# A two-layer diffusion backbone with mixture of experts: order and depth of the expert weight loads

## Chip, cores and metric

The kernel runs on one core of one Trainium2 chip. The metric is the device time of one execution in microseconds (us), the median of several runs.

## What is computed

A latent sequence `x` and a context sequence, 256 tokens of width 1024 each, go through two layers. Each layer mixes tokens with gated recurrences (`token_mix`) and then mixes channels: in layer 0 with a dense SwiGLU, in layer 1 with the two best of eight experts. All of it is float32. The last part, layer 1's channel mix on the 256 latent tokens, is where the change lies:

```python
def swiglu(h, w1, w3, w2):
    return (jax.nn.silu(h @ w1) * (h @ w3)) @ w2

def moe_swiglu(h, router, w1, w3, w2):
    t = h.reshape(b * l, d)
    logits = (t @ router).astype(jnp.float32)
    top_v, top_i = lax.top_k(logits, TOP_K)          # 2 of 8
    top_w = jax.nn.softmax(top_v, axis=-1)
    gates = jnp.sum(jax.nn.one_hot(top_i, N_EXPERTS) * top_w[..., None], axis=1)
    y = jnp.zeros_like(t)
    for e in range(N_EXPERTS):                       # D_EXPERT = 3584
        y = y + gates[:, e:e + 1] * swiglu(t, w1[e], w3[e], w2[e])
```

## The kernel before

Up to about 993 us the kernel does layer 0, layer 1's token mix and its output projection (`w_out`). Then come the experts, to which everything below belongs.

**Experts and steps.** The kernel ranks the experts on the chip by how many tokens chose them; only the expert of rank 0 is fixed beforehand (expert 0). Ranks 1 to 4 are "big" (up to 128 tokens), ranks 0, 5, 6 and 7 "small" (up to 64). An expert's 3584 hidden columns are cut into 7 pieces, so there are 56 steps (r, c), 28 big and 28 small. The list `steps` begins with three small ones (rank 0, pieces 0 to 2), then alternates big and small, and ends with four big ones in a row. The loop at L1233 runs one step n after the other: up projection of step n (`up_big` or `up_small`), `silu` on ACT and the product on DVE (tile `a`), then the down projection of step n-1 (`lower`), then the transposes of `a` on PE. Below, up(n) and lower(n) are these two projections of step n.

**Weights.** A step needs 6 tiles of 1 MB (`w`): four for the up projection, two for the down projection, 336 tiles in all. They are numbered here from 0 in the order in which the plan has them: up(0) has tiles 0 to 3, up(1) 4 to 7, lower(0) 8 and 9, up(2) 10 to 13, lower(1) 14 and 15, up(3), the first big one, 16 to 19. All loads are issued from SP's queue in this order. Each goes into the next buffer of a ring (`raw_ring`, L880) of 12: two of the pool `raws`, which the pieces of `w_out` used before, nine of `pre`, whose memory belonged to layer 1's token mix, and one of `late`. A load waits until what its buffer held has been used, and every load behind it in the queue waits with it. A tile is two pieces. For a small step PE reads the pieces as they are. For a big step each piece is split into a rounded half and a remainder: `wh` on ACT, then `wl` on DVE, into a ring of four pairs of buffers (`spl_ring`).

**Lookahead.** Each engine runs its instructions strictly in the order in which the program issues them. `taken_pieces` decides where in that order loads and splits stand: when PE's work on piece i is issued, the pieces after it are issued too, up to `LOOK` of them or until three split ones stand ahead:

```python
while (len(emitted) <= i or len(emitted) <= i + LOOK and sum(len(x) == 2 for x in emitted[i + 1:]) < 3) \
        and next(feeder, 0) is None:
    pass
```

`EARLY` (L854) is how many pieces of the experts' tiles are issued while `w_out` still runs.

**Gathers.** Tokens are gathered for an expert by matmuls with a one-hot matrix `P`, which DVE builds (`onehot`). For rank 0 this happens ahead of the steps, in the loop at L1027: for each quarter q of the width, `token_lo(q)` makes the remainder half `htkl` of the tokens on DVE, PE gathers, ACT and DVE take the result (`xgs`). Behind the loop `order_experts` computes on DVE which expert has which rank (`whoi`). SP then reads `whoi` into registers with seven TENSOR_LOADs (`read_order`, L998), since the loads of all other ranks take their addresses from there. For the groups of ranks 1 to 4 `open_group(g)` builds `P` at step 0, 11, 25 and 30, and four gathers stand in the down projections that are issued in that step and the three behind it (for group 1, in steps 1 and 2, two each).

Of the kernel before, what the change touches and what calls it, by code (L numbers as in the profile page):

```python
# [27 lines left out]
BIG, SMALL = (1, 2, 3, 4), (0, 5, 6, 7)  # L28
NPRE = 9
AHEAD = 2  # L30
LOOK = 16
EARLY = 1


def body(ctx, tc, I, out, dbg=None):
# [25 lines left out]
    raws = pool("raws", 2)  # L61
# [28 lines left out]
    raw_ring = {"n": 0, "pools": [(raws, 2)]}  # L90
# [720 lines left out]
    pre = pool("pre", NPRE, side="right")  # L811
# [41 lines left out]

    limit[0] = taken[0] + 8 + EARLY - 1  # L854
    w_out(1, 0, to_tokens)
# [21 lines left out]

    mp = pool("mp", 1, side="left")
    late = pool("late", 1, side="left")
    raw_ring.update(n=0, pools=[(raws, 2), (pre, NPRE), (late, 1)])  # L880
    spl_ring.update(n=0, pools=[(spl, 3), (spx, 1)])
    gt = mp.tile([128, 2, NE, NE], F32, name="gt")
    eq = mp.tile([128, 2, NE, NE], F32, name="eq")
# [21 lines left out]
    def token_lo(q):  # L905
        c = slice(256 * q, 256 * q + 256)
        for tt in range(2):
            DVE.scalar_tensor_tensor(htk[1][:, tt, c], x2t[:, tt, c], r2[:, tt:tt + 1], htk[0][:, tt, c].bitcast(F32),
                                     op0=ALU.mult, op1=ALU.subtract)
# [77 lines left out]
    def order_experts():  # L987
        DVE.tensor_copy(cnt, counts)
        DVE.scalar_tensor_tensor(key, cnt, 8.0, seq, op0=ALU.mult, op1=ALU.subtract)
        DVE.memset(key[:, 0:1], 8192.0)  # L990
        DVE.tensor_tensor(cmp_, key[:, None, :].to_broadcast(sq8), key[:, :, None].to_broadcast(sq8), op=ALU.is_gt)
        DVE.tensor_reduce(rk, cmp_, axis=AX.X, op=ALU.add)
        DVE.tensor_tensor(place, rk[:, None, :].to_broadcast(sq8), seq[:, :, None].to_broadcast(sq8), op=ALU.is_equal)
        DVE.tensor_mul(cmp_, place, seq[:, None, :].to_broadcast(sq8))
        DVE.tensor_reduce(who, cmp_, axis=AX.X, op=ALU.add)
        DVE.tensor_copy(whoi, who)
# [27 lines left out]

    xgs[0] = small_tile()
    limit[0] = None
    for q in range(4):  # L1027
        token_lo(q)
        b = bank(("po", "pp")[q % 2])
        for a in range(2):  # L1030
            k = 2 * q + a
            o = b[:, 64 * a:64 * a + 64]
            for i in range(2):
                for tt in range(2):
                    mm(o, htk[i][:, tt, 128 * k:128 * k + 128], hot[0][:, tt, 0:64], i + tt == 0, i + tt == 2)
            if a:
                DVE.tensor_scalar(xgs[0][:, k], o, amp[:, k:k + 1], shift[:, k:k + 1], op0=ALU.mult, op1=ALU.add)
            else:
                ACT.activation(xgs[0][:, k], o, AF.Identity, scale=amp[:, k:k + 1], bias=shift[:, k:k + 1])
    order_experts()  # L1040

    def up_big(ws, xg):
# [93 lines left out]
    def open_group(g):  # L1136
        if len(members(g)) == 2:
            hot[g] = onehot([posr[:, :, g:g + 1], posr[:, :, g + 4:g + 5]], [128, 64])
            xgs[g], xgs[g + 4] = big_tiles(), small_tile()
        else:  # L1140
            hot[g] = onehot([posr[:, :, g:g + 1]], [128])
            xgs[g] = big_tiles()
# [27 lines left out]
    def taken_pieces(n):  # L1170
# [3 lines left out]
        def at(k):  # L1174
            i = first + k
            while (len(emitted) <= i or len(emitted) <= i + LOOK and sum(len(x) == 2 for x in emitted[i + 1:]) < 3) \
                    and next(feeder, 0) is None:
# [1 line left out]
            return tuple(x[:, 0] for x in emitted[i])  # L1179
        return at  # L1180

    before, mids, after = {}, {}, {}

    def at_step(table, n, f):
        table.setdefault(n, []).append(f)
# [7 lines left out]
    n = -5  # L1193
    for g in BIG:
        free = {2: (0,), 3: (1, 5), 4: (2,)}.get(g, ())
        n = max([n + 5] + [1 + steps.index((r, 6)) for r in free])
        assert all(n + (3 if g == 1 else 4) <= steps.index((r, 0)) for r in members(g)), (g, n)
        at_step(before, n, lambda g=g: open_group(g))
        for k in range(0, KT, 2):
            at_step(mids, n + 1 + k // 4 if g == 1 else n + k // 2, lambda g=g, k=k: gather_group(g, k))  # L1200
        at_step(mids, n + 4, lambda g=g: back_group(g))
# [12 lines left out]
    def scatter():  # L1214
        if not jobs:
            return []
        r, t, cuts = jobs.pop(0)
        y = halves(t)
        return [lambda rows=rows, i=i, tt=tt: spill(y, rows, back[r], gate_of(r), i, tt)
                for rows, i in cuts for tt in range(2)]  # L1220
# [12 lines left out]
    for n, (r, c) in enumerate(steps):  # L1233
        if n == len(steps) - 6:
            gf = sb(mp, [128, KT, 128], F32R, "xgh", 2).rearrange("p a b -> p (a b)").bitcast(F32)
            SP.dma_start(gf, I["fg"].partition_broadcast(128))
        rest = scatter()
        a = up_big(taken_pieces(KT), xgs[r]) if r in BIG else up_small(taken_pieces(KT), xgs[r])
        for f in before.pop(n, []):
            f()  # L1240
        rest += mids.pop(n, [])
        if prev is not None:
            lower(*prev, rest)
        prev = (r, c, (turn_big if r in BIG else turn_small)(a))
        for f in after.pop(n, []):
            f()
# [154 lines left out]
```

## Time and profile before

| | |
|---|---|
| Median of 3 runs | 1923.0 us (1922.17 to 1924.91) |
| The profiled execution, its own time | 1919.4 us |
| Its span (first to last instruction) | 1917.6 us |
| PE busy, share of the span | 95 % |
| DVE, ACT busy | 63 %, 50 % |
| DMA, mean over the span | 258 GB/s |

Rows give times from the span's start. PE is TensorE (matmuls), PEld its weight loads, DVE VectorE, ACT ScalarE, POOL GpSimd, SP SyncE, SPq its queue of DMA issues. "[x <-Y]" in a timeline says that the engine stood idle for x us before the instruction and that Y ended it. Matmuls are pipelined, so a busy PE need not be PE at its peak. Most instructions are recorded by one helper, so they all have line L47; the names of the tiles tell them apart.

### The profile page before, as it was taken

The page shows a single profiled execution, that of the slowest core. Times are in us where ns is not written, and L with a number is a line of the kernel's source. Part 1 is how long each engine was busy: PE and PEld are TensorE (multiplying, and loading weights), DVE is VectorE, ACT ScalarE, POOL GpSimd, SP SyncE. Part 2 cuts the span into 40 slices and gives each one's busy share as a digit, 9 for nine tenths or more (in the row PEclk, how much of TensorE's full clock was granted, in tenths as well). Part 3 has the DMA queues.
Part 4 walks back from the last instruction along what each step waited for, and adds up shares of the span by engine and source line. Part 5 has one row for each costly group of instructions (what it writes and reads, how often), then busy time and mean ns, then how long its engine had stood idle before and what let it go on. Part 6 is the DMA issues. An engine that isn't in the chain of part 4 may idle for free.

```text
span 1917.6 us, 30283 instructions
## 1 busy us (share of the span) xinstructions
PE 1830.0 (95%) x11901; PEld 1330.4 (69%) x11901; DVE 1206.3 (63%) x1923; ACT 951.3 (50%) x1506; POOL 49.4 (3%) x94
## 2 busy tenths in 40 slices
PE   6999999999999999999995999999999999999995
PEld 4887778988888888987882466565646565565574
DVE  5799985789774346657751465556646565665485
ACT  4757664532122236666650555444546464454464
POOL 0111100000000001000100000000000000000000
PEclk9999999999999999999998999999999999999998
DMA  9344213366773323311238999999999999999990
GB/s 353 120 148 149 72 47 110 144 229 209 254 269 124 110 95 118 109 45 68 93 107 336 421 422 421 373 405 421 421 408 383 404 396 421 420 421 421 421 412 27
DMA packets 76731, 495.10 MB, mean 258 GB/s; under 512 B 8448, under 2 KB 10752, under 8 KB 23072
## 3 DMA queue, kind: packets, MB, share of 16 engines
q1 hardware_dynamic: 76576, 493.03, 65.4%
q8 instruction: 97, 1.59, 0.3%
q14 instruction: 58, 0.48, 0.1%
HBM read 491.95 MB, written 1.05 MB: 257 GB/s over the span
## 4 chain that ended last, share of the span: by engine, by line
PE 80%; DMA 7%; DVE 6%; ACT 5%; issue 2%; SPq 0%; ACTq 0%; DVEq 0%
PE pj L47 63%; PE po L47 11%; PE pp L47 6%; DMA w<-in_mw 4%; ACT wh L47 1%; ACT kpad L47 1%; DVE junk L47 1%; DMA raw<-in_win 1%; DVE wl L47 1%; ACT ptd L47 1%; DMA wg<-in_wgroup 1%; DMA wm<-in_wmod 1%; DVE Q L47 0%; DVE nt L47 0%; ACT F L47 0%
## 5 line engine op out<-in xcount | busy, mean ns | idle before, releaser
L47 DVE TENSOR_TENSOR wl<-w,wh 128x1024 fp32r<-128x1024 f32 (+1 forms) x501 | 602.1, 1215 | 243.7 <-ACT wh L47 229.2
L47 ACT ACTIVATE wh<-w 128x1024 fp32r<-128x1024 f32 (+1 forms) x501 | 522.3, 1050 | 380.0 <-PE pj L47 279.0
L47 PE MATMUL pj<-hh,wh 128*128 128x512 f32 (+1 forms) x992 | 349.4, 353 | 1.7 <-ACT hh L47 1.0
L47 PE MATMUL pj<-hh,wl 128*128 128x512 f32 (+1 forms) x992 | 347.8, 351 | 1.6 <-DVE wl L47 1.6
L47 PE MATMUL pj<-hl,wh 128*128 128x512 f32 (+1 forms) x992 | 348.7, 352 | 0.5 <-DVE hl L47 0.5
L47 PE MATMUL pj<-w,xgs 128*64 128x512 f32 x896 | 202.5, 603 | 5.8 <-DMA w<-in_mw 5.8
L47 PEld LDWEIGHTS pj<-hh,wh 128*128 128x128 f32 x992 | 186.5, 188 | 30.2 <-issue 3.4
L47 PEld LDWEIGHTS pj<-hl,wh 128*128 128x128 f32 x992 | 186.8, 188 | 27.5 <-issue 2.5
L47 PEld LDWEIGHTS pj<-hh,wl 128*128 128x128 f32 x992 | 186.7, 188 | 26.7 <-DVE wl L47 2.5
L47 DVE SCALAR_TENSOR_TENSOR junk<-wm,cbc 128x1024 bf16<-128x1024 f32 x128 | 156.4, 1222 | 41.1 <-DMA wm<-in_wmod 40.1
L47 PE MATMUL pj<-wh,xgh 128*128 128x512 f32 x448 | 179.8, 401 | 0.0
L47 PE MATMUL pj<-wl,xgh 128*128 128x512 f32 x448 | 177.7, 397 | 0.0
L47 PE MATMUL pj<-wh,xgl 128*128 128x512 f32 x448 | 177.6, 396 | 0.0
L47 DVE TENSOR_TENSOR a<-a,pj 128x256 f32<-128x256 f32 (+1 forms) x78 | 45.8, 589 | 171.6 <-ACT a L47 165.5
L47 PEld LDWEIGHTS pj<-w,xgs 128*64 128x64 f32 x896 | 62.2, 139 | 126.1 <-issue 111.3
L47 ACT ACTIVATE a<-pj 128x256 f32<-128x256 f32 (+1 forms) x78 | 40.0, 513 | 189.8 <-PE pj L47 189.6
L47 PE MATMUL pj<-w,aT 128*64 128x512 f32 x448 | 109.5, 618 | 0.6 <-DMA w<-in_mw 0.6
L47 PEld LDWEIGHTS pj<-wh,xgl 128*128 128x128 f32 x448 | 84.4, 188 | 20.3
L47 PEld LDWEIGHTS pj<-wl,xgh 128*128 128x128 f32 x448 | 84.5, 189 | 19.8 <-DVE wl L47 0.7
L47 PEld LDWEIGHTS pj<-wh,xgh 128*128 128x128 f32 x448 | 84.4, 188 | 19.2
L47 PE MATMUL po<-wh,aTh 128*128 128x512 f32 x224 | 93.3, 417 | 0.7 <-ACT aTh L47 0.7
L47 PE MATMUL po<-wh,aTl 128*128 128x512 f32 x224 | 88.8, 396 | 0.0
(273 smaller groups left out, 2446.7 us busy)
## 6 DMA issues: line engine op xcount, KB each, us to landing
w<-in_mw SPq DMA_DIRECT2D x336, 1024.0 KB, 11.7
wm<-in_wmod SPq DMA_DIRECT2D x80, 512.0 KB, 4.2
w<-in_win SPq DMA_DIRECT2D x31, 1024.0 KB, 4.8
w<-in_fw SPq DMA_DIRECT2D x30, 1024.0 KB, 4.9
w<-in_wout SPq DMA_DIRECT2D x12, 1024.0 KB, 4.8
wg<-in_wgroup SPq DMA_DIRECT2D x8, 1024.0 KB, 14.5
w<-in_fw SPq DMA_DIRECT2D x8, 768.0 KB, 4.3
xT<-in_ctxT SPq DMA_DIRECT2D x1, 1024.0 KB, 8.1
```

The costliest lines, as they stand in the source:

```text
L47: ins = fn(*args, **kw)
```

## The change

Four edits. The ring of 12 buffers begins with the nine of `pre` and not with the two of `raws`. The lookahead is 6 pieces and not 16, and no expert tile is issued while `w_out` runs. `token_lo` runs two quarters ahead of the gathers that need it. And `open_group` of the groups 2 to 4 is issued at the beginning of its step, ahead of the up projection, not behind it.

```diff
--- before.py
+++ after.py
@@ -28,8 +28,8 @@
 BIG, SMALL = (1, 2, 3, 4), (0, 5, 6, 7)
 NPRE = 9
 AHEAD = 2
-LOOK = 16
-EARLY = 1
+LOOK = 6
+EARLY = 0
 
 
 def body(ctx, tc, I, out, dbg=None):
@@ -877,7 +877,7 @@
 
     mp = pool("mp", 1, side="left")
     late = pool("late", 1, side="left")
-    raw_ring.update(n=0, pools=[(raws, 2), (pre, NPRE), (late, 1)])
+    raw_ring.update(n=0, pools=[(pre, NPRE), (late, 1), (raws, 2)])
     spl_ring.update(n=0, pools=[(spl, 3), (spx, 1)])
     gt = mp.tile([128, 2, NE, NE], F32, name="gt")
     eq = mp.tile([128, 2, NE, NE], F32, name="eq")
@@ -1024,8 +1024,9 @@
 
     xgs[0] = small_tile()
     limit[0] = None
+    token_lo(0)
+    token_lo(1)
     for q in range(4):
-        token_lo(q)
         b = bank(("po", "pp")[q % 2])
         for a in range(2):
             k = 2 * q + a
@@ -1037,6 +1038,8 @@
                 DVE.tensor_scalar(xgs[0][:, k], o, amp[:, k:k + 1], shift[:, k:k + 1], op0=ALU.mult, op1=ALU.add)
             else:
                 ACT.activation(xgs[0][:, k], o, AF.Identity, scale=amp[:, k:k + 1], bias=shift[:, k:k + 1])
+        if q < 2:
+            token_lo(q + 2)
     order_experts()
 
     def up_big(ws, xg):
@@ -1179,7 +1182,7 @@
             return tuple(x[:, 0] for x in emitted[i])
         return at
 
-    before, mids, after = {}, {}, {}
+    early, before, mids, after = {}, {}, {}, {}
 
     def at_step(table, n, f):
         table.setdefault(n, []).append(f)
@@ -1195,7 +1198,7 @@
         free = {2: (0,), 3: (1, 5), 4: (2,)}.get(g, ())
         n = max([n + 5] + [1 + steps.index((r, 6)) for r in free])
         assert all(n + (3 if g == 1 else 4) <= steps.index((r, 0)) for r in members(g)), (g, n)
-        at_step(before, n, lambda g=g: open_group(g))
+        at_step(early if n else before, n, lambda g=g: open_group(g))
         for k in range(0, KT, 2):
             at_step(mids, n + 1 + k // 4 if g == 1 else n + k // 2, lambda g=g, k=k: gather_group(g, k))
         at_step(mids, n + 4, lambda g=g: back_group(g))
@@ -1234,6 +1237,8 @@
         if n == len(steps) - 6:
             gf = sb(mp, [128, KT, 128], F32R, "xgh", 2).rearrange("p a b -> p (a b)").bitcast(F32)
             SP.dma_start(gf, I["fg"].partition_broadcast(128))
+        for f in early.pop(n, []):
+            f()
         rest = scatter()
         a = up_big(taken_pieces(KT), xgs[r]) if r in BIG else up_small(taken_pieces(KT), xgs[r])
         for f in before.pop(n, []):
```

What this does to the order on the engines, at three places. First SP's queue, from the last load of `w_out` (`in_wout`) on, before the change; in brackets stands which engine's or DMA queue's count an issue waits for:

```order
L47 DMA w_10063<-in_wout 128x2048 [waits DMAHW1_49,DVE_49]
L47 DMA w_10135<-in_mw 128x2048 [waits DMAHW2_49,DVE_49]
L47 DMA w_10354<-in_mw 128x2048 [waits DMAHW4_49,DVE_49]
L47 DMA w_10356<-in_mw 128x2048 [waits DMAHW5_49,PE_49]
L47 DMA w_10358<-in_mw 128x2048 [waits Pool_49]
L47 DMA w_10360<-in_mw 128x2048 [waits Pool_49]
L47 DMA w_10362<-in_mw 128x2048
L47 DMA w_10364<-in_mw 128x2048 [waits DMAHW3_49]
L47 DMA w_10366<-in_mw 128x2048
```

Four more loads follow until the first TENSOR_LOAD of `whoi`: twelve tiles stand ahead of it. The same queue from the same load on, changed:

```order
L47 DMA w_10063<-in_wout 128x2048 [waits DMAHW1_49,DVE_49]
L47 DMA w_10352<-in_mw 128x2048 [waits Pool_49]
L47 DMA w_10354<-in_mw 128x2048 [waits Pool_49]
L47 DMA w_10356<-in_mw 128x2048
L47 DMA w_10358<-in_mw 128x2048
L47 DMA w_10364<-in_mw 128x2048
L47 DMA w_10370<-in_mw 128x2048 [waits DMAHW2_49]
L47 DMA w_10376<-in_mw 128x2048 [waits DMAHW3_49]
L1000 TENSOR_LOAD whoi [waits DVE_49]
```

The wait for PE, which the third load had, is gone: these tiles all go to `pre`. The first TENSOR_LOAD, which waits for DVE, now stands behind seven tiles.

Second DVE around tile 16, the first that is split; ACT has the halves `wh` of the same pieces at the same places. Before the change (`wl_10527` and `wl_10549` are tile 16, `wl_10573` is tile 17; `xgl` belongs to the gathers of group 1; `a_10520` and `a_10602` are the steps 1 and 2):

```order
L47 TENSOR_TENSOR a_10520<-a_10520,pj_10495 128x256
L47 TENSOR_TENSOR wl_10527<-w_10524,wh_10526 128x1024
L47 TENSOR_TENSOR xgl_10481<-g_10541,xgh_10480 128x256
L47 TENSOR_TENSOR wl_10549<-w_10524,wh_10548 128x1024
L47 TENSOR_TENSOR xgl_10481<-g_10563,xgh_10480 128x256
L47 TENSOR_TENSOR wl_10573<-w_10570,wh_10572 128x1024
L47 TENSOR_TENSOR a_10602<-a_10602,pj_10585 128x256
L47 TENSOR_TENSOR xgl_10481<-g_10616,xgh_10480 128x256
```

The same place, changed (`wl_10585` and `wl_10591` are tile 16, `wl_10602` is tile 17; `a_10510` and `a_10596` are the steps 1 and 2):

```order
L47 TENSOR_TENSOR a_10510<-a_10510,pj_10485 128x256
L47 TENSOR_TENSOR xgl_10471<-g_10527,xgh_10470 128x256
L47 TENSOR_TENSOR xgl_10471<-g_10545,xgh_10470 128x256
L47 TENSOR_TENSOR wl_10585<-w_10582,wh_10584 128x1024
L47 TENSOR_TENSOR wl_10591<-w_10582,wh_10590 128x1024
L47 TENSOR_TENSOR a_10596<-a_10596,pj_10563 128x256
L47 TENSOR_TENSOR wl_10602<-w_10599,wh_10601 128x1024
L47 TENSOR_TENSOR xgl_10471<-g_10616,xgh_10470 128x256
```

The first split of tile 16 stood ahead of all gather results of group 1 and of the transposed `a` of step 1; now it stands behind two of the four and behind `aT` of step 1, ahead of `a` of step 2.

Third DVE in step 11, where group 2 is opened, before the change (`a_11537` is this step's own; `wl_11506` to `wl_11528` are splits for lower(11), the down projection that is issued in the step after):

```order
L47 TENSOR_TENSOR wl_11460<-w_11447,wh_11459 128x1024
L47 TENSOR_TENSOR wl_11472<-w_11469,wh_11471 128x1024
L47 TENSOR_TENSOR wl_11482<-w_11469,wh_11481 128x1024
L47 TENSOR_TENSOR wl_11506<-w_11503,wh_11505 128x1024
L47 TENSOR_TENSOR wl_11516<-w_11503,wh_11515 128x1024
L47 TENSOR_TENSOR wl_11528<-w_11525,wh_11527 128x1024
L47 TENSOR_TENSOR a_11537<-a_11537,pj_11436 128x512
L47 TENSOR_TENSOR P_11540<-con,posr 128x2x128 x2
L47 TENSOR_TENSOR xgl_11544<-g_11557,xgh_11543 128x256
```

The same step, changed (`a_11521` is its own):

```order
L47 TENSOR_TENSOR wl_11421<-w_11418,wh_11420 128x1024
L47 TENSOR_TENSOR P_11435<-con,posr 128x2x128 x2
L47 TENSOR_TENSOR wl_11444<-w_11418,wh_11443 128x1024
L47 TENSOR_TENSOR wl_11456<-w_11453,wh_11455 128x1024
L47 TENSOR_TENSOR wl_11466<-w_11453,wh_11465 128x1024
L47 TENSOR_TENSOR wl_11478<-w_11475,wh_11477 128x1024
L47 TENSOR_TENSOR wl_11488<-w_11475,wh_11487 128x1024
L47 TENSOR_TENSOR a_11521<-a_11521,pj_11442 128x512
L47 TENSOR_TENSOR xgl_11439<-g_11537,xgh_11438 128x256
```

`P` stood behind three splits for the next down projection and behind `a`; it now stands among the splits of its own up projection, and those three splits have gone behind the step's `a`. The move of the three splits repeats in every big step that a small one follows.

## Rows read from the trace of the kernel before

**Rows 1.** Page, the span in 40 slices: DMA share and GB/s of each.

```profile
DMA  9344213366773323311238999999999999999990
GB/s 353 120 148 149 72 47 110 144 229 209 254 269 124 110 95 118 109 45 68 93 107 336 421 422 421 373 405 421 421 408 383 404 396 421 420 421 421 421 412 27
```

**Rows 2.** Page, DMA issues: queue, count, size, median us to landing.

```profile
w<-in_mw SPq DMA_DIRECT2D x336, 1024.0 KB, 11.7
```

**Rows 3.** Windows: length, PE, PEld, DVE, ACT, POOL busy, clock, DMA share, GB/s.

```profile
987.00:1016.00 29.00, 24.25 (x143) 18.36 (x144) 10.82 (x39) 10.51 (x26) 0.00 (x0) 0.82 0.07 27
...
1016.00:1041.60 25.60, 18.23 (x86) 6.26 (x84) 3.40 (x16) 2.41 (x6) 0.00 (x0) 1.00 1.00 413
...
1041.60:1058.30 16.70, 0.64 (x4) 0.00 (x0) 1.23 (x1) 2.38 (x6) 0.00 (x0) 0.61 1.02 423
...
1425.00:1869.00 444.00, 442.38 (x1950) 268.36 (x1950) 267.54 (x269) 227.43 (x279) 0.00 (x0) 1.00 1.00 411
...
1869.00:1917.60 48.60, 29.18 (x119) 21.41 (x117) 28.93 (x35) 22.82 (x31) 0.00 (x0) 0.81 0.08 28
```

**Rows 4.** Timeline, SP's queue: start, us, instruction, count.

```profile
968.39 0.33 SPq L47 DMA_DIRECT2D w<-in_wout  x1
...
977.12 0.33 SPq L47 DMA_DIRECT2D w<-in_mw  x1
...
984.76 0.33 SPq L47 DMA_DIRECT2D w<-in_mw  x1
...
1015.12 7.52 SPq L47 DMA_DIRECT2D w<-in_mw  x10
...
1022.32 5.43 SPq L47 DMA_DIRECT2D w<-in_mw  x3
```

**Rows 5.** Waits of SP's queue, 983 to 1020: total, times, longest us.

```profile
SPq L47 <- PE pj L47: 30.0, 1, 30.0
```

**Rows 6.** Timeline, POOL, 940 to 1000.

```profile
944.22 2.74 POOL L47 COPY ptd<-ptc 32x64 f32<-32x64 f32 x4 [19.78 <-DVE Q L47]
```

**Rows 7.** Timeline, PE, gathers of expert 0 and the first up projection.

```profile
1003.07 0.69 PE L47 MATMUL pp<-P,htkl 128*128 128x64 f32 x2 [0.68 <-DVE htkl L47]
...
1011.71 1.98 PE L47 MATMUL pj<-w,xgs 128*64 128x512 f32 x4
```

**Rows 8.** Timeline, DVE, 999 to 1016.

```profile
1002.54 0.87 DVE L47 SCALAR_TENSOR_TENSOR htkl<-x2t,rsy,htkh 128x256 fp32r<-128x256 f32 x2
...
1013.95 0.17 DVE L47 CAST whoi<-who 128x8 int32<-128x8 f32 x1
```

**Rows 9.** Timeline, PE, steps 0 to 2.

```profile
1019.86 1.51 PE L47 MATMUL pj<-w,xgs 128*64 128x512 f32 x6 [3.07 <-DMA w<-in_mw]
...
1058.32 0.69 PE L47 MATMUL pp<-con,a 128*128 128x128 f32 x2 [16.08 <-ACT xgs L47]
```

**Rows 10.** Timeline, ACT, 1034 to 1062.

```profile
1055.92 1.06 ACT L47 ACTIVATE wh<-w 128x1024 fp32r<-128x1024 f32 x1 [19.98 <-DMA w<-in_mw]
```

**Rows 11.** Chain that ended last, whole run: start, us, what.

```profile
1073.98 14.82 PE pj L47 x64
...
1159.88 13.13 PE pj L47 x56
...
1176.65 7.04 PE pj L47 x32
```

**Rows 12.** Waits, 1065 to 1870: total, times, longest us.

```profile
PE pp L47 <- DVE P L47: 9.0, 3, 4.6
...
ACT wh L47 <- DMA w<-in_mw: 34.5, 22, 7.4
```

**Rows 13.** Waits of SP's queue, 1065 to 1870.

```profile
SPq L47 <- PE pj L47: 299.3, 153, 12.2
```

**Rows 14.** Page, costliest groups: operation, count, busy us, mean ns.

```profile
L47 DVE TENSOR_TENSOR wl<-w,wh 128x1024 fp32r<-128x1024 f32 (+1 forms) x501 | 602.1, 1215 | 243.7 <-ACT wh L47 229.2
...
L47 ACT ACTIVATE wh<-w 128x1024 fp32r<-128x1024 f32 (+1 forms) x501 | 522.3, 1050 | 380.0 <-PE pj L47 279.0
```


## Prediction

> **What bounds the kernel now.** I looked first at the 40 slices for where the copies run. From the 22nd slice to the end the DMA engines are nearly always full, at about 421 GB/s [rows 1]; this is the stage of the experts, with 336 tiles of 1024 KB (1.0486 MB) [rows 2]. A tile at 421 GB/s takes 2.49 us, all of them 837 us. So a time at which this stream stands still is lost, unless PE is the slower one anyway. Then I went through the stage in windows and, for the engine that stood still in each, through its timeline. Three places matter.
>
> The first is a hole in the stream. Between 987 and 1016 us the DMA share is 0.07 [rows 3]. SP issues tile 0 at 977.12, tile 1 at 984.76 and tile 2 only at 1015.12 [rows 4]: it waits 30.0 us for PE [rows 5], since tile 2 goes to the buffer of tile 0, which PE can only read once the gathers for expert 0 are done. The ten loads from 1015.12 on then go out within 7.52 us, into buffers that had long been free; the next row shows the last of them again and two more, with the seven register loads between.
>
> The second is a hole on PE. From 1041.60 to 1058.30 PE is busy for 0.64 us, while the copies run at 423 GB/s [rows 3]. It waits 16.08 us for a gather result (`xgs`) from ACT [rows 9], and ACT waits 19.98 us for a tile [rows 10]: it is the first split of tile 16, issued that early by the lookahead, and all else on ACT stands behind it.
>
> The third is small: in the steps where a group is opened PE waits for `P`, 9.0 us in three waits [rows 12].
>
> From 1425 to 1869 PE is busy for 442.38 of 444 us, with a DMA share of 1.00 [rows 3]. SP often waits for PE there (153 times, 299.3 us) [rows 13], so the ring is full and PE trails the stream. The two are close: a gain must come to both.
>
> **The change, part by part.** The sum is made against the profiled execution, span 1917.6 us, time 1919.4 us; the median of the runs is 3.6 us above that time.
>
> *Ring and seven tiles.* The first load of an expert tile now stands behind the last load of `w_out`, issued at 968.39 [rows 4], and goes to `pre`, whose memory POOL last wrote at 944.22 to 946.96 [rows 6]. Seven tiles take 17.4 us and are there by about 990. Behind them the TENSOR_LOADs wait for `whoi`, and with them every later load, so this wait is new.
>
> *The gather loop.* `whoi` is written at 1013.95 [rows 8], behind four rounds of gathers. In a round PE waits 0.68 us for `htkl` [rows 7], then once more for its second half, 0.44 of 0.87 us [rows 8]. With `token_lo` two rounds ahead three rounds lose these 1.1 us: 3.3 us. Bounds: 0, if ACT and the transit between engines set the round, and 4.9, if PE's granted clock (0.82 in this window [rows 3]) also rises. So `whoi` is there at 1010.8 and up(0) starts at 1008.4 and not 1011.7 [rows 7]. The register loads take at most 4.4 us (5.43 us less three issues of 0.33 [rows 4]): tile 7 is issued at 1015.3. Tile 2 was used 4.74 us after its issue (1015.12 [rows 4] to 1019.86 [rows 9]), so tile 7 lands at 1020.0. Before, it landed five tiles behind tile 2, at 1032.3. **The stream is 12.3 us ahead**; bounds 9.0 and 13.9. EARLY = 0 costs nothing, as tile 0 lands before 980 either way.
>
> *The lookahead at the start.* ACT now stands before two splits of tile 16 and one of tile 17 ahead of the last gather results. Tile 17 lands at 1020.0 + 10 x 2.49 = 1044.9. From the start of the blocking split to PE's transposes it took 2.4 us (1055.92 [rows 10] to 1058.32 [rows 9]), so PE transposes at 1047.3, and up(3) follows at about 1048. PE by itself is no faster: of the 46.6 us from 1011.71 to 1058.32, 16.1 are the wait and 7.4 other idle time (25.60 less 18.23 [rows 3]), so 23.1 us of work lead to 1031.5, and the 15.3 us until the transposes that precede up(3) to 1046.8. Before, up(3) stood at 1073.98 [rows 11]. **PE is 26 us ahead there.** Bounds: 12.3, if PE stays as far behind the stream as now; 28.8, if tile 16 alone holds it (1042.4 + 2.4 + 0.4).
>
> *`P` first.* Two one-hot operations of DVE move ahead of the step's splits; the P buffer was last read by the transposes of the step before, which DVE has passed by then. Of 9.0 us [rows 12] I take **8 us**; bounds 0 and 9.0. Next to come late there are the gather results on ACT.
>
> *The lookahead later on.* Three splits per big step go behind that step's `a` and its transposed copy. They are 1.05 us on ACT and 1.22 us on DVE each [rows 14], in all 4.7 us from the first on ACT to the last on DVE, while PE works 7.04 us on the small up projection between [rows 11]. So I take zero; the cover is 2.3 us, and if it is gone, each big step pays.
>
> *The stream as a limit.* With PE 26 us ahead and the stream 12.3, PE trails less. Tightest is step 9: tile 52 lands at 1020.0 + 45 x 2.49 = 1132.1, PE comes to it at 1159.9 - 26 = 1133.9 [rows 11], and a split needs 2.3 us. I charge **2 us** for this (bounds 0 and 8). Later the gathers slow PE and the distance grows again. At the end the last tile lands at 1020.0 + 328 x 2.49 = 1837, 32 us before 1869, where the copies now end [rows 3]; this agrees with PE's gain.
>
> Sum: 26 + 8 - 2 = **32 us**. The profiled execution would take 1887.4 us, and the median, 3.6 above, **1891 us**.
>
> **The rivals.**
>
> *The stream alone decides.* PE's hole from 1041.6 to 1058.3 is covered by the copies, which run at 423 GB/s in it [rows 3], and in the stage as a whole they are full. If PE is again pushed back by the stream, only the 12.3 us remain: 1910.7 us. For it speaks that ACT still waits for tiles in 22 places [rows 12]; against it that SP waits 299.3 us for PE's reads [rows 13], so the ring is full and PE the one waited for, and that 48.6 us of work come after the last copy [rows 3]; so it has the lesser chance. The Trainium skill (Perfetto Trace Analysis, Identifying the Most-Contended Engine) says that kernels gain by improving the engine with the highest utilization, for DMA the share of the memory's bandwidth; and (Roofline) that a core which streams alone tops out at about 120 % of 358 GB/s, by estimate 430. By these two this rival would hold, as the copies are near their ceiling and PE's hole lies beside them; the trace agrees on the rate (421 GB/s [rows 1]).
>
> *Everything comes off.* up(3) is 28.8 us earlier, `P` brings 9.0, and the stream charges nothing: 38 us, 1885 us.
>
> *The splits come too late* (slower). If PE waits at the down projection of each big step for its first split, 1.05 + 1.22 = 2.3 us [rows 14] in each of 25 big steps that a small one follows, 57 us stand against 32: 1948 us. It decides from 1.3 us per step on. Against it stand the 2.3 us of cover above; for it, that DVE has `a` and other work between.
>
> *Nothing changes.* If the first seven loads are held until `w_out` and the gathers are over, and then the register loads, the hole stays, and with it the time: 1923 us. POOL's row [rows 6] speaks against it.
>
> **How the numbers follow.** Forecast 0.67, stream alone 0.13, everything 0.10, too late 0.06, nothing 0.04. The range takes in the first three with the bounds of their terms, 0.90 of the chance: from 1880 us (everything, the gather loop at its bound, 1.6 us more, and the 1.6 us that PE still stands between 1425 and 1869 [rows 3], with two for the spread of the runs) to 1912 us (the stream alone and its spread). A difference of 0.2 % (3.8 us) is about what a measurement can tell from none: faster 0.90, same 0.04, slower 0.06.
>
> **What would show it.** In the profile after: seven loads right behind 968 us and a DMA share of full from about 1015 on; `whoi` at about 1011; ACT waiting for tile 16 until about 1042, but PE not over 2 us for gather results; up(3) at about 1048; no wait of PE for `P`; the copies' end near 1837. It is wrong if PE waits for `wl` at the down projections, if the stream does not start before 1015, or if PE still trails by as much and the copies stop for it.

## The result and the profile after

The changed kernel takes **1887.4 us** (median of 4 runs, 1886.19 to 1892.01). The kernel before, run beside it, takes 1922.6 us (4 runs, 1918.7 to 1924.91). The ratio is 0.9823 with a 95 % interval of 0.9800 to 0.9847, a gain of 35 us. Predicted were 1891 us and a gain of 32 us. The profiled execution went from a span of 1917.6 us to one of 1885.1 us, 32.5 us less. The total was well met; the experiments show that its terms were not what I took them for.

The slices of the page after, which answer to [rows 1]:

```profile
DMA  9344212456774324311264999999999999999991
GB/s 359 110 161 136 90 47 90 157 201 216 262 268 148 106 79 140 110 50 68 78 255 186 421 422 421 421 422 421 421 420 421 421 421 421 421 420 422 421 412 41
```

The dips of before (373, 383, 396 GB/s) are gone. The windows (length, PE, PEld, DVE, ACT, POOL busy, clock, DMA share, GB/s), for [rows 3]:

```profile
987.00:1016.00 29.00, 25.98 (x160) 18.33 (x160) 10.82 (x39) 10.72 (x26) 0.00 (x0) 0.88 0.12 47
1016.00:1041.60 25.60, 24.65 (x122) 9.33 (x118) 4.25 (x18) 6.19 (x17) 0.00 (x0) 1.00 1.00 413
...
1425.00:1837.00 412.00, 410.28 (x1816) 249.86 (x1815) 249.97 (x249) 211.24 (x257) 0.00 (x0) 1.00 1.01 420
1837.00:1885.10 48.10, 28.18 (x116) 20.68 (x115) 28.39 (x35) 22.38 (x31) 0.00 (x0) 0.82 0.13 46
```

The hole in the copies is still there (DMA share 0.12 from 987 to 1016), but seven tiles lie ahead of it. The copies end at about 1840 (DMA share 0.65 from 1837 to 1840, 0.10 from 1840 to 1845), a little later than the forecast 1837. SP's queue, for [rows 4]:

```profile
968.64 0.33 SPq L47 DMA_DIRECT2D w<-in_wout  x1
969.31 3.46 SPq L47 DMA_DIRECT2D w<-in_mw  x7
...
1015.01 7.66 SPq L47 DMA_DIRECT2D w<-in_mw  x10
```

Its waits from 983 to 1020 (total, times, longest us), for [rows 5]. SP now waits for `whoi`, as the order said:

```profile
SPq L1000 <- DVE whoi L47: 38.0, 1, 38.0
```

The end of the gather loop on PE and `whoi` on DVE, for [rows 7] and [rows 8]. No round waits for `htkl` any more:

```profile
1007.34 0.64 PE L47 MATMUL pp<-P,htkh 128*128 128x64 f32 x2 [0.49 <-ACT xgs L47]
...
1008.33 4.18 PE L47 MATMUL pj<-w,xgs 128*64 128x512 f32 x12
```

```profile
1010.58 0.17 DVE L47 CAST whoi<-who 128x8 int32<-128x8 f32 x1
```

The first split of tile 16 on ACT ([rows 10]) and what PE does then ([rows 9]):

```profile
1043.42 2.00 ACT L47 ACTIVATE wh<-w 128x1024 fp32r<-128x1024 f32 x2 [11.34 <-DMA w<-in_mw]
```

```profile
1048.35 0.44 PE L47 MATMUL pp<-con,a 128*128 128x128 f32 x2 [3.69 <-DVE wl L47]
1048.55 0.63 PE L47 MATMUL pj<-wh,xgh 128*128 128x512 f32 x1
```

ACT still waits 11.34 us for the tile, but it comes 12.5 us earlier than before (1043.42 and not 1055.92 [rows 10]; 12.3 were forecast), and PE works on for steps 0 to 2 meanwhile, until 1044.66. Up(3) starts at 1048.55. In the chain that ended last its piece stands at 1048.79 and not at 1073.98 [rows 11], 25.2 us earlier:

```profile
1048.79 16.35 PE pj L47 x64
```

All waits of PE from 1040 to 1840, for [rows 12], where 9.0 us for `P` stood:

```profile
PE pp L47 <- DVE wl L47: 3.7, 1, 3.7
PE pp L47 <- DVE a L47: 1.4, 1, 1.4
PE po L47 <- DVE wl L47: 0.9, 2, 0.7
PE pp L47 <- DVE x2t L47: 0.8, 1, 0.8
PE pj L47 <- DVE wl L47: 0.2, 1, 0.2
```

And SP's from 1040 to 1840, for [rows 13]. It now waits more for copies (an issue waits until an earlier load has landed) than for PE: the stream has become nearly as tight as PE.

```profile
SPq L47 <- DMA w<-in_mw: 298.0, 177, 2.4
SPq L47 <- PE pj L47: 192.9, 107, 5.8
```

This table shows where the time lies: us from PE's first matmul on one tile to its first on another, in the timeline of PE. "Look 16" is experiment 3 below, "16 tiles" experiment 10. Differences in the text are taken before rounding.

| tiles | before | changed | look 16 | 16 tiles |
|---|---|---|---|---|
| 0 to 16, up(3) | 62.0 | 40.2 | 38.4 | 36.6 |
| 16 to 66 | 121.4 | 123.1 | 123.5 | 120.0 |
| 66 to 72, group 2 opens | 22.1 | 14.6 | 14.7 | 14.6 |
| 72 to 78 | 19.4 | 23.4 | 19.4 | 19.4 |
| 78 to 144 | 161.1 | 161.1 | 161.1 | 161.1 |
| 144 to 156, group 3 opens | 35.2 | 29.7 | 29.7 | 29.7 |
| 156 to 300 | 363.9 | 362.1 | 362.8 | 362.1 |
| 300 to 312 | 25.9 | 27.4 | 25.9 | 25.9 |
| 312 to 334 | 66.0 | 66.5 | 66.0 | 66.0 |

From tile 16 to 334 the changed kernel gains 7.3 us (815.1 to 807.8): 13.1 won where groups 2 and 3 open and 1.8 from 156 to 300, 7.6 lost in four other rows. One of these is 72 to 78. There the profile shows PE in step 11 (start, us, instruction):

```profile
1193.49 0.39 PE L47 MATMUL po<-wh,aTl 128*128 128x512 f32 x1
1194.67 0.73 PE L47 MATMUL pp<-y,PTa 64*128 64x512 f32 x2 [0.79 <-DVE x2t L47]
1195.34 0.68 PE L47 MATMUL po<-wh,aTh 128*128 128x512 f32 x1
1195.81 0.63 PE L47 MATMUL po<-wl,aTh 128*128 128x512 f32 x1
...
1202.36 0.39 PE L47 MATMUL po<-wh,aTh 128*128 128x512 f32 x1
```

Behind a short stand a matmul of 512 columns takes 0.63 us and not 0.39 until 1202: PE runs at half clock, the lower of its two levels (1.2 and 2.4 GHz); the granted clock from 1195 to 1202.4 is 0.54. The same is to be seen behind the 3.69 us ahead of up(3), whose first eight matmuls take 0.63 us. Busy time doesn't show this; the rows' durations do.

### The profile page after: what moved, and what is told of

The parts are those of the page before. It is cut to its first block, busy times and chain, and to the rows that moved or that the text cites. A ratio compares the mean times of both kernels' runs of the same rounds, so it can differ in the third digit from the quotient of the medians.

```text
span 1885.1 us, 30248 instructions
## 1 busy us (share of the span) xinstructions
PE 1825.1 (97%) x11901; PEld 1329.5 (71%) x11901; DVE 1203.9 (64%) x1923; ACT 947.7 (50%) x1506; POOL 49.4 (3%) x94
## 4 chain that ended last, share of the span: by engine, by line
PE 77%; DMA 8%; DVE 6%; ACT 6%; issue 2%; SPq 0%; ACTq 0%; DVEq 0%
PE pj L47 61%; PE po L47 11%; DMA w<-in_mw 7%; PE pp L47 6%; DVE wl L47 1%; ACT wh L47 1%; ACT kpad L47 1%; DVE junk L47 1%; DMA wm<-in_wmod 1%; ACT ptd L47 1%; DMA xT<-in_xT 1%; DVE Q L47 0%; DVE nt L47 0%; ACT F L47 0%; DVE hl L47 0%
## 5 line engine op out<-in xcount | busy, mean ns | idle before, releaser
L47 PE MATMUL po<-wl,aTh 128*128 128x512 f32 x224 | 89.8, 401 | 0.9 <-DVE wl L47 0.9
```

Source lines behind the costliest of these rows:

```text
L47: ins = fn(*args, **kw)
```

## The experiments

Differences between kernels of different rounds are given by their ratios to the kernel before, run beside each.

### 1. Ring and EARLY alone

```diff
-EARLY = 1
+EARLY = 0
...
-    raw_ring.update(n=0, pools=[(raws, 2), (pre, NPRE), (late, 1)])
+    raw_ring.update(n=0, pools=[(pre, NPRE), (late, 1), (raws, 2)])
```

> The kernel before with the ring order of the change and EARLY = 0, lookahead 16, nothing else. Seven is the number of tiles ahead of the register loads only with a lookahead of 6; with 16 there are twelve, all for rank 0 and rank-0 buffers that are free by then, so the copies should run on through most of 970 to 1000. The first load behind the registers, tile 12, goes out at about 1013.95 (whoi) + 4.5 = 1018.5 and lands at 1023.2, where before it landed at 1019.86 + 10 x 2.49 = 1044.8: the stream is 21.6 us ahead. ACT's first split of tile 16 stands ahead of the gather results as before, but tile 16 lands at 1033.2, when PE's own 23.1 us of work from 1011.7 (to 1034.8) are not yet over. Own theory (PE's place at the first big step is set by the later of ACT's blocking split and PE's own work, and the rest of the run keeps the shift): PE transposes at about 1037, up(3) at about 1052 and not 1074, time 1901 us (gain 22). Rival, the stream alone decides: 21.6 us, the same time. Second rival, the lookahead itself costs (ACT stands before splits that are issued too early, wherever the tiles are): only the 9 us that the prediction gave the ring without the gather loop, 1913 us.

Measured: 1899.3 us, ratio 0.9884 (0.9862 to 0.9906), 21.5 us. In its profile tiles 0 to 16 take 38.6 us, where before they take 62.0; the three waits for `P` are still 9.1 us. Own theory held, the second rival fell. The first rival, that the stream alone decides, forecast the same time; this run can't tell it from the theory, experiment 2 does. What I had not seen when I predicted: with a lookahead of 16 twelve tiles and not seven stand ahead of the register loads. So the short lookahead makes the lead smaller that this edit gives.

### 2. The lookahead alone

```diff
-LOOK = 16
+LOOK = 6
```

> The kernel before with a lookahead of 6 and nothing else. The stream does not move: tile 2 is still issued at about 1015 behind PE's wait, five tiles in flight cover the register loads, tile 16 lands at about 1055 and tile 17 at 1057. But two gathers' results and the transposed a of step 1 stand ahead of the first blocking split on ACT. Own theory: PE does its work up to the transposes of step 2 while ACT waits for the tile; after the blocking split at 1055.9 the transposes follow 4.8 us later as in the changed kernel (1043.42 to 1048.23), at 1060.7, and up(3) directly behind them at 1061.3, where before 15.3 us of work still came between: 12.7 us earlier than 1073.98. Step 9 then needs tile 52 at 1144.4 + 2.3 = 1146.7 and PE comes at 1147.2, so it is kept: 1910 us. Rival, the stream alone decides: no gain, 1923 us. If the three splits behind a come too late in each big step: slower than 1923.

Measured: 1900.7 us, ratio 0.9900 (0.9874 to 0.9926), 20.0 us: 7 us more than I expected, and no room for the rival. SP's waits from 975 to 1030, PE at the end of its hole, and PE's wait for `P` from 1067 to 1855:

```profile
SPq L47 <- PE pj L47: 30.3, 1, 30.3
```

```profile
1063.57 0.44 PE L47 MATMUL pp<-con,a 128*128 128x128 f32 x2 [3.65 <-ACT xgs L47]
```

```profile
PE pp L47 <- DVE P L47: 1.7, 3, 0.6
```

The stream stands as long as before, so it didn't move. Tiles 0 to 16 take 49.7 us, 12.3 less than before: this is the expected part. The rest comes from `P`: with the short lookahead the three splits that stood ahead of it on DVE are gone, and its waits fall from 9.0 to 1.7 us. Where groups 2 and 3 open that brings 11.8 us, of which 4.8 are lost again from tile 16 to 66 and from 300 to 312, where PE waits for `a`. My expectation had left both out.

### 3. The change with the lookahead of 16

```diff
-LOOK = 6
+LOOK = 16
```

> The changed kernel with the lookahead back at 16 (ring order, gather loop and one-hot matrices as changed). Twelve tiles stand ahead of the register loads again, so the stream should be ahead by five tiles, 12.4 us, more than in the changed kernel: tile 12 issued at 1015, tile 16 landing at about 1029.7, before PE's own work for steps 0 to 2 is over (1031.5). Own theory: ACT's early split then blocks nobody, up(3) stands at 1048 to 1050 as in the changed kernel, and the time is within 4 us of it, 1887 us. Rival, the lookahead itself is worth 13.7 us of the 26 (26 less the 12.3 of the stream) wherever the tiles are: 1901 us. Rival, the stream alone decides: faster than the changed kernel by up to 12 us, 1875 us.

Measured: 1882.4 us, ratio 0.9796 (0.9775 to 0.9817). The interval touches that of the changed kernel (0.9800 to 0.9847), the median is 5 us better. That is 1 us beyond the 4 that I gave it, and neither rival's number: 1901 us is out, and of the 12 us that a stream so much earlier would be worth by itself at most half came. So with the ring's edit in place the short lookahead shows no gain. By the table above it rather costs: PE's half-clock stretches and the losses at 72 to 78 and 300 to 312 are not there, against 1.8 us more inside the row 16 to 66 (tiles 42 to 60: 44.8 us against 43.0).

### 4. The change with P late

```diff
-        at_step(early if n else before, n, lambda g=g: open_group(g))
+        at_step(before, n, lambda g=g: open_group(g))
```

> The changed kernel with the one-hot matrices of groups 2 to 4 behind the up projection of their step, as before the change; all else as changed. Own theory: PE waits again for P in three steps, 8 us together (bounds 0 and 9.0), up(3) stays at about 1048.8, and the time is 1895 us. Rival, the stream alone decides, so that a wait of PE is made up behind it: 1887 us as in the changed kernel. With the short lookahead only DVE's own a stands ahead of P and not three splits, so a smaller wait, 3 us and 1890 us, would say that the lookahead had already brought most of it.

Measured: 1889.3 us, ratio 0.9833 (0.9813 to 0.9854), which can't be told from the changed kernel. PE's wait for `P` is 1.7 us in three waits. The last sentence of the expectation was the right one: once the lookahead is 6, moving `P` is worth some 2 us at most. In the profile the three places where groups 2 to 4 open take 0.6 to 0.7 us longer each than in the changed kernel.

### 5. P early, alone

The kernel before, with these lines alone:

```diff
-        at_step(before, n, lambda g=g: open_group(g))
+        at_step(early if n else before, n, lambda g=g: open_group(g))
...
+        for f in early.pop(n, []):
+            f()
         rest = scatter()
```

> The kernel before with the one-hot matrices of groups 2 to 4 at the beginning of their step, and nothing else. Own theory, formed from the runs so far: a wait of PE for P costs more than its row, since PE then runs at half clock for a while: in the kernel before tiles 66 to 78 take 41.6 us from first use to first use and 34.1 us in the kernel with the change and lookahead 16, tiles 144 to 156 35.2 and 29.7, tiles 180 to 192 33.0 and 32.2. All three off: 13.8 us, 1909 us. Rival, as the prediction had it: the waits' own 9.0 us at most, less what comes late next, 8 us: 1914.6 us. Up(3) stays at about 1074 either way.

Measured: 1909.2 us, ratio 0.9941 (0.9929 to 0.9954), which is 8.8 to 13.6 us; the 8 us of the prediction's term (1914.6 us) lie just outside. The profile is clearer: tiles 16 to 334 take 801.5 us and not 815.1, 13.6 less. PE's timeline shows why the wait's row is not its price. Before:

```profile
1206.56 0.71 PE L47 MATMUL pp<-P,htkh 128*128 128x192 f32 x2 [4.60 <-DVE P L47]
...
1208.49 4.83 PE L47 MATMUL pj<-w,aT 128*64 128x512 f32 x12
```

With `P` early:

```profile
1207.18 0.47 PE L47 MATMUL pp<-P,htkh 128*128 128x192 f32 x2
...
1208.25 2.79 PE L47 MATMUL pj<-w,aT 128*64 128x512 f32 x12
```

The same twelve matmuls take 2.0 us more behind the wait. The 4.60 us of the row cost 7.4 us from tile 66 to 72 (22.1 and 14.7).

### 6. Idle matmuls in the place of the wait

The kernel before; `gather` gets a number of idle matmuls to issue first.

```diff
+        b = bank("pp")
+        idle(filler, b)
...
+        gather(..., 32 if k == 0 and g in (2, 3) else 0)
```

> The kernel before with 32 idle matmuls of 128 columns on PE ahead of the first gather of groups 2 and 3, in the place where PE waits for P (4.6 us and about 4). They change no wait: P comes when it came. Own theory on the clock: what follows the wait runs at half clock because PE stood (12 small down matmuls took 4.83 us after it, 2.80 us without the wait), so with PE kept at work they take 2.8 us at a granted clock of 1.00; 2 us come off at each of the two places and the time falls by 4 us, to 1918.5 us. Rival, the half clock there has another cause: the rows behind the wait stay at 4.8 us, and the time is 1922.6 us.

Measured: 1923.2 us, ratio 1.0005 (0.9993 to 1.0018): no gain. The clock's part came out, the time's did not:

```profile
1204.18 7.41 PE L47 MATMUL pp<-con 128*128 128x128 f32 x64
1211.35 0.45 PE L47 MATMUL pp<-P,htkh 128*128 128x192 f32 x2
...
1212.39 2.79 PE L47 MATMUL pj<-w,aT 128*64 128x512 f32 x12
```

Two windows, before and here; the granted clock stands ahead of the DMA share. From 1205 to 1210 PE at first stands before the edit, and runs idle matmuls here; from 1210 to 1215 follow rows from behind the wait:

```profile
1205.00:1210.00 5.00, 3.44 (x12) 2.32 (x14) 1.42 (x4) 1.40 (x5) 0.00 (x0) 0.58 1.02 421
1210.00:1215.00 5.00, 5.00 (x20) 1.62 (x18) 2.02 (x4) 1.11 (x3) 0.00 (x0) 0.74 0.85 297
```

```profile
1205.00:1210.00 5.00, 5.00 (x48) 5.00 (x47) 3.57 (x5) 1.54 (x2) 0.00 (x0) 1.00 1.02 421
1210.00:1215.00 5.00, 5.00 (x35) 3.06 (x33) 0.43 (x1) 1.70 (x5) 0.00 (x0) 1.00 0.78 300
```

`P` comes when it came, and the rows behind it run at full clock: PE's stand is what brings the half clock there. But the 32 idle matmuls, 64 in the records, last 7.41 us and not about 4.6, and `P` was done at 1208.69 (its row on DVE: 1207.94, 0.75 us), so PE came 2.7 us late to it and the gain was given back.

The Trainium skill (Perfetto Trace Analysis, Matmul Optimizations) says that TensorE scales its power with its utilization, so that matmuls should follow each other without gaps. The durations in these rows agree (4.83 us against 2.79).

### 7. EARLY alone

```diff
-EARLY = 1
+EARLY = 0
```

> The kernel before with EARLY = 0 and nothing else: ring in its old order, lookahead 16. Own theory: the hole in the copies came from the one early tile, on whose buffer tile 2 fell. Tiles 0 and 1 now wait for the last splits of w_out (977 and 985 us), the ten behind them go out at once and land by about 1014, some 12 tiles ahead of the register loads; from there on as in the kernel with ring and EARLY changed (1899.3 us): 1899 us. Rival, as the prediction put it, that the ring's order is what lets the loads go out: the order is old, so no gain, 1922 us.

Measured: 1898.5 us, ratio 0.9880 (0.9861 to 0.9899): all that experiment 1 gave, with the ring in its old order, so the rival is out. Tiles 0 to 16 take 38.6 us in both. SP's queue from 968 to 990:

```profile
976.13 12.98 SPq L47 DMA_DIRECT2D w<-in_mw  x10
```

### 8. The change with the ring in its old order

The changed kernel with one line undone:

```diff
-    raw_ring.update(n=0, pools=[(pre, NPRE), (late, 1), (raws, 2)])
+    raw_ring.update(n=0, pools=[(raws, 2), (pre, NPRE), (late, 1)])
```

> The changed kernel with the ring in its old order (raws first); EARLY stays 0. Own theory: the hole in the copies before the change came from the one tile that was issued early: its buffer was counted from the ring's old start, so that tile 2 fell on it and waited for PE. Without the early tile, tiles 0 and 1 wait for the splits of w_out (977 and 985 us) and tiles 2 to 6 follow at once into pre; all seven are there by about 1003, before up(0) at 1008. The order of the ring then brings nothing: 1887 us, within 2 us of the changed kernel. Rival, as the prediction put it (the ring begins with buffers that are free, which lets the seven loads go out at 968): the old order costs the 12.3 us of the stream or a part of it, 1893 to 1900 us.

Measured: 1890.2 us, ratio 0.9835 (0.9818 to 0.9852), 2.8 us above the changed kernel by the medians (2.3 by the ratios) and up to 0.8 beyond what I expected, but its interval overlaps the changed kernel's widely. All seven loads go out by 988.5, and tiles 0 to 16 take the same 40.2 us:

```profile
977.83 10.64 SPq L47 DMA_DIRECT2D w<-in_mw  x7
```

So it is the tile issued early that made the hole at 987: the ring was counted anew behind it, and tile 2 fell on its buffer. Without it the order of the ring brings nothing that can be measured. What this profile has more lies far behind, from tile 300 to 312 (33.0 us and not 27.4, 72 to 78 has 3.0 less). There ACT waits 10.57 us for a tile that is to be split, `a` stands behind that split, and PE waits 4.4 us for `a`: the same hold as ahead of up(3), late in the run:

```profile
1780.67 2.00 ACT L47 ACTIVATE wh<-w 128x1024 fp32r<-128x1024 f32 x2 [10.57 <-DMA w<-in_mw]
1782.58 0.36 ACT L47 ACTIVATE a<-pj 128x256 f32<-128x256 f32 x1
```

Whether the new order alone, with the early tile, would do as well was not tried.

### 9. token_lo in its old place

The changed kernel with this edit undone:

```diff
-    token_lo(0)
-    token_lo(1)
     for q in range(4):
+        token_lo(q)
...
-        if q < 2:
-            token_lo(q + 2)
```

> The changed kernel with token_lo in its old place, ahead of each quarter's gathers. Own theory: three rounds of the gather loop get their 1.1 us back, whoi and with it the register loads and tile 7 come 3.2 us later behind the loop's beginning, up(0) 3.3 us later: 1890.6 us. Rival, ACT and the transit between the engines set the round: 1887 us, the rounds as long as in the changed kernel.

Measured: 1893.0 us, ratio 0.9853 (0.9836 to 0.9869), 5.7 us above the changed kernel. From the last `w_out` load to up(0) it is 43.4 us (968.04 to 1011.47) and 39.7 in the changed kernel (968.64 to 1008.33): 3.7 us for the loop, where 3.3 were said. The other 2 us come later: tiles 300 to 312 take 32.5 us there, with a 4.4 us wait of PE for `a` and a half-clock stretch behind it, while 72 to 78 take 20.3. They aren't the price of this edit: experiment 8 has 33.0 and 20.4 in the same rows, with `token_lo` in its new place.

### 10. Sixteen tiles ahead of the register loads

The changed kernel, with the loads that need no register issued before the registers are read.

```diff
     def read_order():
+        while len(emitted) < taken[0] - KT + 32 and next(feeder, 0) is None:
+            pass
         for r in range(1, NE):
```

> The changed kernel, but in step 0 the loads of sixteen tiles (all that need no register) are issued ahead of the seven register loads, and not seven; lookahead 6 as changed. Own theory: with a lookahead of 6 what is left to win lies in the places where the stream is still too late: the hole on PE ahead of up(3) (4.3 us, and 1.9 us in which PE then ran at half clock), the waits behind splits near steps 9 to 11 and 50 to 52 (about 3 us) and the half-clock stretch at 1195 to 1202 (3 us). Tiles 7 to 11 go out from 973 to 1000, tile 12 at about 1011, tile 16 at about 1020. No gap in the copies except from about 1000 to 1010; no wait of PE for xgs or wl ahead of up(3); the time is 1878 us (1875 to 1881). Rival, PE is already the limit and the waits only move: 1887 us as the changed kernel. Rival, the whole gain of lookahead 16 in the kernel with all else changed came from the later steps and not from its twelve tiles: 1885 us.

Measured: **1876.4 us**, ratio 0.9769 (0.9751 to 0.9787), clear of the changed kernel's interval. Three windows, the last over nearly the whole stage, and the only wait of PE that the view lists from 1014 to 1830:

```profile
987.00:1016.00 29.00, 25.98 (x159) 18.23 (x160) 10.81 (x39) 10.73 (x26) 0.00 (x0) 0.88 0.65 262
...
1041.60:1048.20 6.60, 6.60 (x34) 4.28 (x33) 2.45 (x5) 5.30 (x13) 0.00 (x0) 1.00 1.02 419
...
1016.00:1825.00 809.00, 807.92 (x3598) 487.25 (x3595) 479.80 (x498) 415.26 (x527) 0.00 (x0) 1.00 1.01 420
```

```profile
PE pp L47 <- DVE a L47: 0.9, 1, 0.9
```

The hole ahead of up(3) is closed, PE is busy for 807.92 of 809 us, and the granted clock of the stage is 1.00: the stretch at 1195 is gone too. So in the changed kernel these losses came from a stream that ran too close to PE.

### 11. The same with the lookahead of 16

Experiment 10, and:

```diff
-LOOK = 6
+LOOK = 16
```

> The same sixteen tiles ahead of the register loads, with the lookahead of 16. Only tiles 12 to 15 differ from the kernel with the change and lookahead 16, which stood at 1882.4 us. Own theory: there PE lost 1.6 us to a late gather result ahead of up(3) and nothing to the stream, so the four tiles bring at most 2 us, and the three splits ahead of a still cost 1.9 us in steps 6 to 9: 1881 us, slower than with lookahead 6 and sixteen tiles by about 3 us. Rival, the longer lookahead is better in itself once the tiles are there: 1877 us, and the kernel with lookahead 6 is the slower one.

Measured: 1882.2 us, ratio 0.9798 (0.9766 to 0.9830). As expected it is no better than with twelve tiles. With lookahead 6 the median is 5.8 us better, though the intervals overlap a little. The profiles point the same way: tiles 36 to 60 take 59.3 us here and 56.9 with lookahead 6, and PE waits 3.7 us in four waits for `a`, which stands behind the early splits. So the short lookahead seems to pay once the tiles are there; the times alone don't settle it.

### 12. A bank for each gather

Experiment 10, and in the gather loop of expert 0:

```diff
-        b = bank(("po", "pp")[q % 2])
         for a in range(2):
             k = 2 * q + a
-            o = b[:, 64 * a:64 * a + 64]
+            o = bank(("po", "pp")[a])[:, 0:64]
```

> The kernel with sixteen tiles ahead of the register loads and lookahead 6, and in the gather loop for expert 0 each eighth of the width gets a bank of its own, so that PE does not write a bank that ACT reads. Own theory: the four waits of PE for xgs in the loop (0.49 us each) go, 2 us, and PE, which stands less, keeps its clock longer, up to 2 us more: 1873.5 us (1872 to 1875). Rival, DVE sets the round then (token_lo and the evictions): PE waits for htkl in the place of xgs, 1876 us as without the edit.

Measured: **1872.4 us**, ratio 0.9746 (0.9734 to 0.9759), the best of all, 48 us under the kernel before by the medians (1920.7 and 1872.4) and within the range that I gave. Against experiment 10 the intervals overlap a little; the profiles place the gain in the loop: from the last `w_out` load to up(0) it is 36.2 us and not 39.7, and the tiles behind take the same time. PE in the last round, in experiment 10 and here:

```profile
1006.30 0.61 PE L47 MATMUL pp<-P,htkl 128*128 128x64 f32 x2
1007.41 0.64 PE L47 MATMUL pp<-P,htkh 128*128 128x64 f32 x2 [0.49 <-ACT xgs L47]
```

```profile
1006.02 0.39 PE L47 MATMUL po<-P,htkh 128*128 128x64 f32 x2
1006.25 0.40 PE L47 MATMUL po<-P,htkl 128*128 128x64 f32 x2
1006.63 0.41 PE L47 MATMUL pp<-P,htkh 128*128 128x64 f32 x2
```

The waits for `xgs` are gone and the rows stay at 0.4 us and not 0.6. The Trainium skill (Perfetto Trace Analysis, Matmuls) says that independent groups of matmuls should rotate through banks, so that one is emptied while the next is filled; the 0.49 us agree.

## Why the prediction was right, and where it was not

**The stream's hole, right in time, not in cause.** Tile 7 was to be issued at 1015.3 and was at 1015.01, and tile 16 came 12.5 us earlier, where 12.3 were said. I gave this to the ring's order and to seven tiles ahead. Experiments 7 and 8 show that EARLY = 0, which I had costed at nothing, does it by itself, and experiments 1 and 3 that seven is the smaller number: without the short lookahead it is twelve.

**The gather loop, right.** `whoi` at 1010.58 (said 1010.8), up(0) at 1008.33 (said 1008.4); undone, it costs 3.7 us in the loop (said 3.3).

**The lookahead at the start, right for this kernel.** Up(3) stands 25.2 us earlier, 26 were said. The step that was off is PE's wait, 3.7 us where I had none over 2 (PE's own work was over at 1044.66, 2 us before the 1046.8 of my sum, and the tile came 1 us later than in it), and the half clock behind it, which I had not thought of. And the term is no property of the lookahead: ring and EARLY alone (EARLY by itself, experiment 7) bring up(3) nearer to up(0) by 23.4 us (62.0 to 38.6), the lookahead alone by 12.3. Both work on one cause, a split on ACT that waits for a tile not there yet: one makes the tile come earlier, the other puts the split later. Their gains can't be added.

**`P` first, wrong in two ways.** "Of 9.0 us I take 8" was mis-sized: alone the edit is worth 11.5 us between the medians and 13.6 in the profile, since PE runs at half clock behind the two long waits (4.60 and 3.88 us). And in this change it was worth some 2 at most, since the lookahead takes the same three splits from ahead of `P` (experiments 2 and 4).

**The stream as a limit, mis-sized.** I charged 2 us. The table shows 7.6: 1.7 from tile 16 to 66, 4.0 from 72 to 78, 1.4 from 300 to 312, 0.5 behind. How the loss falls between 72 to 78 and 300 to 312 differs from profile to profile with seven tiles ahead and lookahead 6 (4.0 and 1.4 here, 1.0 and 7.1 in experiment 8), so each figure is that of one execution. Experiment 10, which moves nothing but loads, wins all of it back and 1.4 us more, and 3.6 us ahead of up(3).

**The sum.** 25.2 at the start for 26, 14.9 where groups open and from 156 to 300 for 8, 7.6 of losses for 2: 32.5 us for 32. Two errors of some 6 us each, both in good part from the half clock behind PE's stands, cancelled; that the total came out so close is luck.

**The lookahead later on, right.** I took zero for the splits behind `a`, and PE waits only 0.9 us for `wl` at the down projections in the whole stage.

**The rivals.** *The stream alone decides* fell: the lookahead alone leaves the stream where it was and brings 20 us. The Trainium skill's rule (Perfetto Trace Analysis, Identifying the Most-Contended Engine) would have given this rival's time; here the copies were near their ceiling, and yet most of the gain came from PE's stands. *The splits come too late* and *nothing changes* fell by the result. *Everything comes off*, 1885 us, was a little nearer to the measured time than the forecast (2.4 us and 3.6), but its condition, that the stream charges nothing, did not hold.

## What to carry to other kernels

A queue that runs in order loses time at the first instruction in it that isn't ready, so ask for each load and each split both what stands behind it and what would have to be there for it to start; two edits at one such place don't add up. Issue what needs no late information (here sixteen loads) ahead of the instruction that waits for it. And price a stand of PE by the durations behind it too, not by its wait alone: 4.6 us of waiting cost 7.4 us.

## What was not expected of the hardware

Behind a stand PE can fall to half clock, and the rows behind stay at 0.63 us for 512 columns for 3 us (up(3)) to 6 (experiment 4 from 1785 on) more. But the length of the stand alone doesn't tell whether it falls. In the changed kernel it fell behind 0.79 us (1194.67), for 7 us; in experiment 8 it stood longer in the same place and did not fall:

```profile
1195.22 0.73 PE L47 MATMUL pp<-y,PTa 64*128 64x512 f32 x2 [0.89 <-DVE x2t L47]
1195.88 0.50 PE L47 MATMUL po<-wh,aTh 128*128 128x512 f32 x1
1196.22 0.39 PE L47 MATMUL po<-wl,aTh 128*128 128x512 f32 x1
```

The half clock is the larger part of what 72 to 78 lost: 23.4 us in the changed kernel, 20.4 in experiment 8, 19.4 before. Elsewhere PE fell behind stands of 1.97 us (experiment 2, 1022.63), 2.29 (experiment 9, 1051.35) and 3.7 to 4.6, and did not behind 3.07 (before, 1019.86 [rows 9], granted clock 1.00 from 1016 to 1041.6 [rows 3]) or 2.97 (experiment 2, 1799.27). What tips it stays open. With sixteen tiles ahead it did not fall anywhere from 1016 to 1825.
